# The up projection of the feed-forward layer by seven products instead of eight (hybrid encoder, one core)

## The chip, the cores and the metric

One core of one Trainium2 chip runs the whole program. The metric is the time of one execution on the device, in microseconds (us); lower is better. TensorE (PE in the rows) multiplies matrices, VectorE (DVE), ScalarE (ACT) and GpSimd (POOL) work element by element, SyncE (SP) issues the DMAs. SBUF is the memory next to the engines, PSUM the small one that TensorE writes.

## The reference

Two layers of an encoder with 512 tokens and 1024 features. Each layer has a mixer (three attention branches with gates), and after it a feed-forward part, the one that is changed:

```python
h = rms_norm(x, norm_ffn[l])
x = x + jnp.square(jax.nn.relu(h @ w_ff1[l])) @ w_ff2[l]
```

`w_ff1` is 1024 x 4096 (the up projection), `w_ff2` is 4096 x 1024 (the down projection), all in float32.

## The kernel before, in words

Activations stand feature-major: a tile has 128 features by 512 tokens. Precision is kept by splitting every operand in two: `hi` is the value rounded to the type float32r, `lo` the rest, and a product is three matmuls (hi·hi, hi·lo, lo·hi) that add up in one PSUM bank (`feature_tile`, L331). Each matmul has its own load of 128x128 weights and streams 512 columns.

Weights come through `Stream.take`: one DMA of 512 KB into `raw`, a copy on ScalarE that makes `whi` (L140), a subtraction on VectorE that makes `wlo` (L142). There are three buffers of each.

`merge` makes the output projection: eight tiles `ps_o` of 24 matmuls. As each is done, `x` takes it up (L908), `norm_part` multiplies it by the gain and splits it into `xgh` and `xgl` (L271, L272), and `norm_square` adds its square to `acc` (ScalarE L282, GpSimd L283). The factor per token of the norm is applied later, after the up projection.

`ffn` then runs two halves. A half makes 16 tiles of the up projection (`up`, 24 matmuls each), evacuates each with relu and the factor `rb` (L930), squares it and splits it into `ah` and `al` (L933 to L935), and then makes eight tiles of the down projection, of 48 matmuls each, that are added to `x` (L964). In the first half the sums of the norm (`norm_sums`, `ps_sum`) and its row (`norm_rows`, `ps_r`) are put between the first up tiles.

TensorE runs in the order in which the program is written. The order on the other engines is set by a scheduler from priorities and from a model of when each instruction is ready; `high_priority(30)` moves the making of weights some 30 instructions ahead. Every engine then runs its instructions strictly in that order.

## Time and profile before

| | |
|---|---|
| runs of the kernel | 1854.17, 1857.88 (median), 1862.26 us |
| profiled execution | 1858.96 us, its span 1856.9 us |
| TensorE busy | 1801.5 us, 97% of the span, 8496 matmuls |
| VectorE busy | 1088.9 us, 59% |
| ScalarE busy | 784.5 us, 42% |
| GpSimd busy | 311.4 us, 17% |
| granted TensorE clock | 0.993 of full speed (2.4 GHz) |

The span goes from the first to the last instruction. Busy time of TensorE counts a matmul from its start to its modelled end, so that neighbours overlap; how fast matmuls follow each other is read from their starts, or from a stretch that holds nothing else, divided by their number.

### The profile page before, as it was taken

How to read it: one execution, taken by the hardware profiler on the slowest of the kernel's cores; microseconds unless marked ns; L12 is line 12 of the kernel's file. 1: busy time of each engine (PE TensorE's matmuls, PEld its weight loads, DVE VectorE, ACT ScalarE, POOL GpSimd, SP SyncE). 2: the span in 40 equal slices, each digit the busy share in tenths (PEclk: the TensorE clock that was granted, in tenths of full speed). 3: DMA queues.
4: the chain of work that ended last, by engine and by line, in shares of the span. 5: the costliest groups of instructions: out<-in, count | busy, mean ns of one | idle time of the engine just before them, and what ended most of it. 6: DMA issues, size and time to landing. Idle time of an engine off the chain costs nothing.

```text
span 1856.9 us, 23295 instructions
## 1 busy us (share of the span) xinstructions
PE 1801.5 (97%) x8496; PEld 1495.0 (81%) x8496; DVE 1088.9 (59%) x2223; ACT 784.5 (42%) x1369; POOL 311.4 (17%) x289
## 2 busy tenths in 40 slices
PE   8989989989999999999999899899899999999999
PEld 6778878877888888888887788788778888888887
DVE  7566468488865642454355654684888756334632
ACT  6565456446643221223245644564466433222221
POOL 1442222043101000000124312220431110000000
PEclk9999999999999999999999999999899999999999
DMA  5653365332252333333336533643322533333341
GB/s 180 154 147 105 101 163 138 100 113 69 80 193 80 106 99 98 96 100 110 119 113 158 132 96 109 169 116 110 103 84 80 178 95 97 102 91 102 92 119 62
DMA packets 78850, 211.46 MB, mean 114 GB/s; under 512 B 11392, under 2 KB 14464, under 8 KB 78736
## 3 DMA queue, kind: packets, MB, share of 16 engines
q1 hardware_dynamic: 78736, 209.97, 39.3%
q8 instruction: 67, 1.10, 0.2%
q14 instruction: 47, 0.39, 0.1%
HBM read 172.15 MB, written 12.62 MB: 100 GB/s over the span
## 4 chain that ended last, share of the span: by engine, by line
PE 79%; DVE 8%; ACT 4%; DMA 4%; issue 3%; POOL 2%; SPq 1%; DVEq 0%; ACTq 0%; POOLq 0%
PE ps L331 38%; PE ps_t L366 15%; PE ps_f L331 10%; PE ps_o L331 5%; PE ps_b L776 5%; PE ps_s L662 2%; PE ps_p L689 2%; PE ps_y L700 2%; DMA qq<-nat 2%; DVE pr L677 1%; POOL wlo L142 1%; DVE pr L670 1%; ACT whi L140 1%; DMA cb<-cum 1%; ACT pr L675 1%
## 5 line engine op out<-in xcount | busy, mean ns | idle before, releaser
L140 ACT ACTIVATE whi<-raw 128x1024 fp32r<-128x1024 f32 (+1 forms) x337 | 307.1, 919 | 764.8 <-issue 320.6
L142 DVE TENSOR_TENSOR wlo<-raw,whi 128x1024 fp32r<-128x1024 f32 (+2 forms) x237 | 287.6, 1213 | 232.2 <-ACT whi L140 227.8
L331 PE MATMUL ps<-xgh,whi 128*128 128x512 f32 x512 | 199.4, 389 | 0.0
L331 PE MATMUL ps<-xgh,wlo 128*128 128x512 f32 x512 | 199.2, 389 | 0.0
L331 PE MATMUL ps<-xgl,whi 128*128 128x512 f32 x512 | 199.2, 389 | 0.0
L331 PE MATMUL ps<-ah,whi 128*128 128x512 f32 x512 | 199.2, 389 | 0.0
L331 PE MATMUL ps<-al,whi 128*128 128x512 f32 x512 | 199.2, 389 | 0.0
L331 PE MATMUL ps<-ah,wlo 128*128 128x512 f32 x512 | 199.2, 389 | 0.0
L331 PE MATMUL ps_f<-xgh,whi 128*128 128x512 f32 x464 | 196.2, 423 | 0.0
L331 PE MATMUL ps_f<-xgh,wlo 128*128 128x512 f32 x464 | 182.5, 393 | 0.0
L331 PE MATMUL ps_f<-xgl,whi 128*128 128x512 f32 x464 | 182.5, 393 | 0.0
L142 POOL TENSOR_TENSOR wlo<-raw,whi 128x1024 fp32r<-128x1024 f32 x50 | 121.1, 2422 | 257.0 <-ACT whi L140 234.3
L366 PE MATMUL ps_t<-whi,xgh 128*128 128x512 f32 x384 | 151.2, 394 | 7.0 <-ACT whi L140 7.0
L366 PE MATMUL ps_t<-wlo,xgh 128*128 128x512 f32 x384 | 150.1, 391 | 0.0
L366 PE MATMUL ps_t<-whi,xgl 128*128 128x512 f32 x384 | 149.9, 390 | 0.0
L283 POOL TENSOR_TENSOR acc<-acc,t 128x512 f32<-128x512 f32 x24 | 41.6, 1732 | 518.9 <-ACT t L282 518.9
L331 PEld LDWEIGHTS ps<-ah,whi 128*128 128x128 f32 x512 | 96.1, 188 | 20.1
L331 PEld LDWEIGHTS ps<-xgl,whi 128*128 128x128 f32 x512 | 96.1, 188 | 19.9
L331 PEld LDWEIGHTS ps<-xgh,wlo 128*128 128x128 f32 x512 | 96.1, 188 | 19.9
L331 PEld LDWEIGHTS ps<-al,whi 128*128 128x128 f32 x512 | 96.1, 188 | 19.9
L331 PEld LDWEIGHTS ps<-xgh,whi 128*128 128x128 f32 x512 | 96.1, 188 | 19.9
L331 PEld LDWEIGHTS ps<-ah,wlo 128*128 128x128 f32 x512 | 96.1, 188 | 19.8
(194 smaller groups left out, 3387.0 us busy)
## 6 DMA issues: line engine op xcount, KB each, us to landing
raw<-w SPq DMA_DIRECT2D x277, 512.0 KB, 3.6
qq<-nat SPq DMA_DIRECT2D x64, 128.0 KB, 2.9
kk<-nat SPq DMA_DIRECT2D x64, 128.0 KB, 2.4
kl<-nat SPq DMA_DIRECT2D x64, 128.0 KB, 2.4
gd<-t SPq DMA_DIRECT2D x32, 256.0 KB, 2.2
cb<-cum SPq DMA_DIRECT2D x16, 256.0 KB, 4.0
cb<-gd SPq DMA_DIRECT2D x16, 256.0 KB, 2.7
g<-gd SPq DMA_DIRECT2D x16, 256.0 KB, 4.3
```

The source lines that it names most:

```text
L140: nc.scalar.activation(out=hi[:, c : c + v], in_=raw[:, c : c + v], func=AF.Copy)
L142: k.lo_engine.tensor_tensor(out=lo[:, c : c + w], in0=raw[:, c : c + w], in1=hi[:, c : c + w].bitcast(F32), op=ALU.subtract)
L283: (engine or nc.gpsimd).tensor_tensor(out=self.acc, in0=self.acc, in1=sq, op=ALU.add)
L331: nc.tensor.matmul(out=ps, lhsT=a[:, k], rhs=b[k], start=first and k == 0 and j == 0, stop=last and k == n - 1 and j == 2)
L366: nc.tensor.matmul(out=pss[t][:, 0:width], lhsT=a[k][:, t * P : t * P + P], rhs=b[:, i], start=c == 0 and i == 0 and j == 0, stop=last and ...
L662: nc.tensor.matmul(out=ps[:, 0:n], lhsT=a[:, i * P : (i + 1) * P], rhs=b[:, 0:n], start=j == 0, stop=j == len(terms) - 1)
L670: nc.vector.tensor_tensor_reduce(out=p, in0=ps[:, 0:n], in1=b, scale=1.0, scalar=-3e38 * sign, op0=ALU.add, op1=ALU.max if branch == 2 els ...
L675: nc.scalar.activation(out=p, in_=p, func=AF.Exp, bias=mn, scale=sign, accum_out=ls)
L677: nc.vector.tensor_scalar(out=p, in0=p, scalar1=li, scalar2=None, op0=ALU.mult)
L689: nc.tensor.transpose(ps[:, o + (i - kb) * P : o + (i - kb + 1) * P], pr[:, offs[i] + kb * P : offs[i] + (kb + 1) * P], self.ident)
L700: nc.tensor.matmul(out=yps[:, kb * P : T], lhsT=qkv[2][kb // 2][:, kb % 2, h, :], rhs=head[h][gi][x][:, o : o + T - kb * P], start=gi == 0 ...
L776: nc.tensor.matmul(out=pss[u], lhsT=chunk[a][:, u, k], rhs=y[b][k], start=k == 0 and j == 0, stop=k == 3 and j == 2)
```

## The change

The up projection is done for two tiles (256 output features) at once by Strassen's scheme in Winograd's form: the contraction of 1024 is cut into two halves of 512, the outputs into two tiles of 128, the tokens into two halves of 256. Where eight block products were needed, seven are made, from sums and differences of the blocks, and their results are added up again.

- Weights (`take_pair`): two DMAs of 512 KB bring the four blocks. GpSimd makes four differences of 128x512 (`t1` to `t4`). Seven blocks are split into hi and lo: ScalarE makes one copy of 512 columns (`b11`, in buffers of its own) and three of 1024, VectorE as many subtractions.
- Activations (`norm_pair`, in `merge`): the tiles kt and kt + 4 are paired, and the eight output tiles run in the order 0, 4, 1, 5, 2, 6, 3, 7. For each pair VectorE makes the sums `s1` to `s4` in halves of 256 tokens, and everything is split in hi and lo.
- Products (`pair_products`): 7 x 4 x 3 = 84 matmuls of 256 columns with 128x128 weights each, into four PSUM banks that hold two results each; two sets of four banks alternate. The first pair of a layer runs part by part of the contraction, the others product by product.
- Sums (`pair_sum`): ScalarE copies one result of 256 columns from PSUM, VectorE makes four additions, each with one operand in PSUM, of 512, 512, 256 and 512 columns. ScalarE then makes relu, square and the hi copy of 1024 columns, VectorE the subtraction for lo.
- The factor of the norm is squared and applied after the down projection (one more VectorE operation for each of its tiles). The two halves become four blocks of four pairs: 336 matmuls of 256 columns, then eight down tiles of 24 matmuls.

The number of bytes loaded stays the same.

```diff
--- before.py
+++ after.py
@@ class Stream @@
+    def take_pair(self, pool, *key):
+        k, nc = self.k, self.k.nc
+        raw = [k.pw.tile([P, 1024], F32, tag="raw", name="raw") for _ in range(2)]
+        sums = [pool.tile([P, 1024], F32, tag="tw", name="tw", bufs=2) for _ in range(2)]
+        w = {}
+        def split(names, src, n, tags):
+            hi, lo = (p.tile([P, n], F32R, tag=t, name=t, **b) for p, t, b in tags)
+            nc.scalar.activation(out=hi[:, 0:n], in_=src[:, 0:n], func=AF.Copy)
+            nc.vector.tensor_tensor(out=lo[:, 0:n], in0=src[:, 0:n], in1=hi[:, 0:n].bitcast(F32), op=ALU.subtract)
+            for i, name in enumerate(names):
+                w[name] = tuple(x[:, 512 * i : 512 * i + 512].rearrange("p (k m) -> p k m", m=P) for x in (hi, lo))
+        with k.tc.high_priority(k.ahead):
+            for i in range(2):
+                nc.sync.dma_start(out=raw[i], in_=self.ap[self.layer, :, self.at + 1024 * i : self.at + 1024 * i + 1024])
+            b = [raw[i][:, 512 * j : 512 * j + 512] for i in range(2) for j in range(2)]
+            t = [sums[i][:, 512 * j : 512 * j + 512] for i in range(2) for j in range(2)]
+            sub = lambda out, x, y: nc.gpsimd.tensor_tensor(out=out, in0=x, in1=y, op=ALU.subtract)
+            plain = ((k.pw, "whi", {}), (k.pw, "wlo", {}))
+            summed = ((pool, "twh", dict(bufs=2)), (pool, "twl", dict(bufs=2)))
+            split(["b11"], raw[0], 512, ((pool, "bh", dict(bufs=2)), (pool, "bl", dict(bufs=2))))
+            split(["b21", "b22"], raw[1], 1024, plain)
+            sub(t[0], b[1], b[0])
+            sub(t[1], b[3], t[0])
+            split(["t1", "t2"], sums[0], 1024, summed)
+            sub(t[2], b[3], b[1])
+            sub(t[3], b[2], t[1])
+            split(["t3", "t4"], sums[1], 1024, summed)
...
@@ class Kern @@
+    def norm_pair(self, l, vcol, pool, kt, x):
+        nc = self.nc
+        h2 = T // 2
+        a, b = slice(0, h2), slice(h2, T)
+        g = self.gain(l, vcol + kt)
+        if kt < 4:
+            self.half = self.half if kt else {}
+            t = self.half[kt] = self.tmp()
+            nc.scalar.activation(out=t, in_=x, func=AF.Copy, scale=g)
+            return
+        t = self.half.pop(kt - 4)
+        q = pool.tile([P, 3, h2], F32, tag="sq", name="sq", bufs=1)
+        sub = lambda out, u, v: nc.vector.tensor_tensor(out=out, in0=u, in1=v, op=ALU.subtract)
+        h = self.px.tile([P, T], F32R, tag="xgh", name="xgh")
+        lo = self.px.tile([P, T], F32R, tag="xgl", name="xgl")
+        nc.scalar.activation(out=h, in_=x, func=AF.Copy, scale=g)
+        sub(q[:, 1], t[:, a], t[:, b])
+        nc.vector.scalar_tensor_tensor(out=t[:, b], in0=x[:, b], scalar=g, in1=t[:, b], op0=ALU.mult, op1=ALU.add)
+        sub(q[:, 0], t[:, b], t[:, a])
+        nc.vector.scalar_tensor_tensor(out=q[:, 2], in0=x[:, a], scalar=g, in1=q[:, 0], op0=ALU.mult, op1=ALU.subtract)
+        nc.vector.scalar_tensor_tensor(out=lo, in0=x, scalar=g, in1=h.bitcast(F32), op0=ALU.mult, op1=ALU.subtract)
+        f = {"a12": [y[:, a] for y in (h, lo)], "a22": [y[:, b] for y in (h, lo)]}
+        h = self.px.tile([P, T], F32R, tag="xgh", name="xgh")
+        lo = self.px.tile([P, T], F32R, tag="xgl", name="xgl")
+        nc.scalar.activation(out=h, in_=t, func=AF.Copy)
+        sub(lo, t, h.bitcast(F32))
+        f |= {"a11": [y[:, a] for y in (h, lo)], "s1": [y[:, b] for y in (h, lo)]}
+        h = pool.tile([P, 3, h2], F32R, tag="sh", name="sh", bufs=4)
+        lo = pool.tile([P, 3, h2], F32R, tag="sl", name="sl", bufs=4)
+        nc.scalar.activation(out=h, in_=q, func=AF.Copy)
+        sub(lo, q, h.bitcast(F32))
+        for i in range(3):
+            f[f"s{2 + i}"] = [y[:, i] for y in (h, lo)]
+        self.xf.append(f)
...
@@ def merge @@
-                self.norm_part(l, V_FFN, m, x[m])
-            outs = [out(m) for m in range(KT)]
+                self.norm_pair(l, V_FFN, pool, m, x[m])
+                self.norm_square(m, x[m])
+            self.xf = []
+            outs = [out(m) for m in (0, 4, 1, 5, 2, 6, 3, 7)]
...
+    PRODUCTS = (
+        ("b11", "a11", 0, 0),
+        ("b21", "a12", 1, 0),
+        ("t2", "s2", 1, 1),
+        ("t3", "s3", 2, 0),
+        ("t1", "s1", 2, 1),
+        ("t4", "a22", 3, 0),
+        ("b22", "s4", 3, 1),
+    )
+    def pair_products(self, w, tags, steps):
+        nc = self.nc
+        h2 = T // 2
+        ps = [None] * 4
+        n = len(self.xf)
+        for i, k in steps:
+            stationary, moving, bank, half = self.PRODUCTS[i]
+            if ps[bank] is None:
+                ps[bank] = self.bank(tags[bank], f"ps_w{bank}")
+            out = ps[bank][:, half * h2 : half * h2 + h2]
+            hi, lo = w[stationary]
+            xh, xl = self.xf[k][moving]
+            for j, (a, b) in enumerate(((hi, xh), (hi, xl), (lo, xh))):
+                nc.tensor.matmul(out=out, lhsT=a[:, k], rhs=b, start=k == 0 and j == 0 and i in (0, 1, 3, 5), stop=k == n - 1 and j == 2 and i in (0, 2, 4, 6))
+            yield
+        self.ps = ps
+    def pair_sum(self, ps, z):
+        nc = self.nc
+        h2 = T // 2
+        add = lambda out, x, y: nc.vector.tensor_tensor(out=out, in0=x, in1=y, op=ALU.add)
+        two = lambda x: x.rearrange("p (u t) -> p u t", u=2)
+        p1 = self.tmp()[:, 0:h2]
+        nc.scalar.activation(out=p1, in_=ps[0][:, 0:h2], func=AF.Copy)
+        add(z[:, 0:5:4], two(ps[1]), p1.unsqueeze(1).to_broadcast([P, 2, h2]))
+        add(z[:, 5:7], two(ps[2]), z[:, 4].unsqueeze(1).to_broadcast([P, 2, h2]))
+        add(z[:, 3], ps[2][:, h2:T], z[:, 5])
+        add(z[:, 1:3], two(ps[3]), z[:, 5:7])
+        return z[:, 0:4].rearrange("p (u v) t -> p u (v t)", u=2)
@@ def ffn @@
     def ffn(self, l, x):
         nc = self.nc
         with ExitStack() as ctx:
+            pa = self.pool(ctx, "act", 4)
+            pf = self.pool(ctx, "ffn", 1)
+            take = lambda j: self.streams[l].take_pair(pf, "f1", j)
+            def up(j, w, a):
+                steps = [(i, k) for k in range(4) for i in range(7)] if j == 0 else [(i, k) for i in range(7) for k in range(4)]
+                yield from self.pair_products(w, (("y", "mm", "mm", "mm"), ("s", "s", "pt", "pt"))[j % 2], steps)
+                c = self.pair_sum(self.ps, pf.tile([P, 7, T // 2], F32, tag="z", name="z"))
+                nc.scalar.activation(out=c, in_=c, func=AF.Relu)
+                nc.scalar.activation(out=c, in_=c, func=AF.Square)
+                h, lo = pa.tile([P, 2, T], F32R, tag="ah", name="ah"), pa.tile([P, 2, T], F32R, tag="al", name="al")
+                nc.scalar.activation(out=h, in_=c, func=AF.Copy)
+                nc.vector.tensor_tensor(out=lo, in0=c, in1=h.bitcast(F32), op=ALU.subtract)
+                for u in range(2):
+                    a[0].append(h[:, u])
+                    a[1].append(lo[:, u])
+            def down(q, m, a):
+                ps = self.mm.tile([P, T], F32, tag="mm", name="ps_2")
+                w = self.streams[l].take(1024, "f2", 8 * q, m)
+                yield from self.feature_tile(ps, [c.rearrange("p (k m) -> p k m", m=P) for c in w], *a)
                 t = self.tmp()
+                nc.vector.tensor_tensor(out=t, in0=ps, in1=rb2, op=ALU.mult)
+                nc.vector.tensor_tensor(out=x[m], in0=x[m], in1=t, op=ALU.add)
+                if q == 3:
+                    if l + 1 < DEPTH:
+                        nc.sync.dma_start(out=self.xd[:, m], in_=x[m])
+                        self.norm_part(l + 1, V_MIX, m, x[m])
+                    else:
+                        nc.sync.dma_start(out=self.a["out"][:, m], in_=x[m])
+            w = take(0)
+            for q in range(4):
                 a = ([], [])
+                for j in range(4 * q, 4 * q + 4):
+                    ahead = take(j + 1) if j % 4 < 3 else None
+                    run_all(up(j, w, a))
+                    w = ahead
+                    if j == 0:
+                        self.norm_sums()
+                    if j == 1:
+                        self.norm_rows("mm")
+                        rb2 = self.rb
+                        nc.vector.tensor_tensor(out=rb2, in0=rb2, in1=rb2, op=ALU.mult)
+                if q == 3 and l + 1 < DEPTH:
                     self.norm_begin()
+                downs = [down(q, m, a) for m in range(KT)]
+                for d in downs[0:2]:
+                    for _ in range(6):
+                        next(d)
+                for i, d in enumerate(downs):
+                    if i == 5 and q < 3:
+                        w = take(4 * q + 4)
+                    run_all(d)
...
@@ def chunk_of @@
-        c = pk(i["w_ff1"][l][:, key[1] * P : (key[1] + 1) * P])
+        w = i["w_ff1"][l][:, 2 * key[1] * P : (2 * key[1] + 2) * P]
+        c = np.stack([pk(w[512 * r : 512 * r + 512, P * u : P * u + P]) for r in range(2) for u in range(2)], axis=1)
```

## Rows read from the trace of the kernel before

**Rows 1.** The page of the profile: its span, the busy time of each engine with its share of the span and instructions, and the shares by engine in the chain that ended last.

```profile
span 1856.9 us, 23295 instructions
PE 1801.5 (97%) x8496; PEld 1495.0 (81%) x8496; DVE 1088.9 (59%) x2223; ACT 784.5 (42%) x1369; POOL 311.4 (17%) x289
...
PE 79%; DVE 8%; ACT 4%; DMA 4%; issue 3%; POOL 2%; SPq 1%; DVEq 0%; ACTq 0%; POOLq 0%
```

**Rows 2.** Busy time by stretch: the stretch and its length, then busy us (and instructions) of TensorE, its weight loads, VectorE, ScalarE and GpSimd, the granted clock, the share of the DMA engines and GB/s. In order: first up half, first down half, second up half, second down half of layer 0, and the output projection before them; then the last down half of layer 1.

```profile
578.80:667.38 88.58, 88.58 (x395) 73.29 (x394) 53.47 (x85) 26.53 (x34) 1.79 (x1) 1.00 0.32 95
667.38:754.42 87.04, 87.04 (x385) 72.10 (x384) 26.39 (x26) 17.54 (x18) 0.00 (x0) 1.00 0.32 97
754.42:841.46 87.04, 87.04 (x385) 72.10 (x384) 50.09 (x62) 24.74 (x31) 0.00 (x0) 1.00 0.32 97
841.46:928.50 87.04, 87.04 (x385) 72.10 (x384) 31.04 (x33) 25.43 (x31) 10.78 (x6) 1.00 0.37 115
...
1765.99:1853.20 87.21, 87.20 (x385) 71.88 (x383) 23.95 (x24) 15.38 (x15) 0.00 (x0) 1.00 0.29 88
535.28:578.80 43.52, 43.52 (x194) 36.05 (x192) 23.37 (x28) 17.55 (x24) 10.30 (x6) 1.00 0.35 103
```

**Rows 3.** The timeline of TensorE in a run of matmuls of 384 columns (start in us, time from the first start to the last end, instruction, x how many merged): three starts of the same kind, three matmuls apart.

```profile
376.48 0.51 PE L366 MATMUL ps_t<-whi,st 128*128 128x384 f32 x2
...
377.00 0.51 PE L366 MATMUL ps_t<-whi,st 128*128 128x384 f32 x2
...
377.52 0.51 PE L366 MATMUL ps_t<-whi,st 128*128 128x384 f32 x2
```

**Rows 4.** The timeline of TensorE where three matmuls of 256 columns stand in a row, each with weights of its own, and the start of the matmul behind them.

```profile
440.42 0.52 PE L662 MATMUL ps_s<-st 96*128 96x256 f32 x3
440.78 0.39 PE L331 MATMUL ps_f<-xgh,whi 128*128 128x512 f32 x1
```

**Rows 5.** The weight loads of one group of matmuls (busy us, mean ns of one).

```profile
L331 PEld LDWEIGHTS ps<-xgh,whi 128*128 128x128 f32 x512 | 96.1, 188 | 19.9
```

**Rows 6.** Groups of ScalarE by shape (busy us, mean ns of one, idle before): copies of 1024, 512 and 768 columns, an evacuation of 256 columns from PSUM, and a load of the function table.

```profile
L140 ACT ACTIVATE whi<-raw 128x1024 fp32r<-128x1024 f32 x227 | 240.6, 1061 | 716.8 <-issue 314.4 <-PE ps L331 238.9 <-PE ps_t L366 97.0
L140 ACT ACTIVATE whi<-raw 128x512 fp32r<-128x512 f32 x102 | 61.1, 622 | 27.1 <-PE ps_t L366 20.3 <-issue 6.2 <-DMA raw<-w 0.5
L691 ACT ACTIVATE pth<-ps_p 128x256 fp32r<-128x256 f32 x48 | 17.8, 371 | 10.4 <-PE ps_p L689 10.1
L140 ACT ACTIVATE whi<-raw 128x768 fp32r<-128x768 f32 x4 | 3.4, 846 | 8.0 <-PE ps_t L366 4.4 <-PE ps_f L331 3.7
L432 ACT ACT_TABLE_LOAD x2 | 2.6, 1283 | 0.0
```

**Rows 7.** Groups of VectorE by shape: subtractions of 1024, 512 and 768 columns with both operands in SBUF, and operations with one operand in PSUM on 512 and 256 columns.

```profile
L142 DVE TENSOR_TENSOR wlo<-raw,whi 128x1024 fp32r<-128x1024 f32 x227 | 280.1, 1234 | 224.6 <-ACT whi L140 220.2 <-DMA raw<-w 2.2 <-DMA cb<-rel 2.2
L142 DVE TENSOR_TENSOR wlo<-raw,whi 128x512 fp32r<-128x512 f32 x2 | 1.4, 692 | 0.3 <-ACT whi L140 0.3
L142 DVE TENSOR_TENSOR wlo<-raw,whi 128x768 fp32r<-128x768 f32 x4 | 3.8, 958 | 7.2 <-ACT whi L140 7.2
L964 DVE TENSOR_TENSOR x<-x,ps 128x512 f32<-128x512 f32 x32 | 22.0, 687 | 113.4 <-PE ps L331 113.4
L692 DVE TENSOR_TENSOR ptl<-ps_p,pth 128x256 fp32r<-128x256 f32 x48 | 20.1, 418 | 11.5 <-ACT pth L691 11.2
```

**Rows 8.** Timelines of GpSimd and VectorE in four places where both work: around 405, 550, 386 and 426 us (start us, us, instruction).

```profile
405.14 2.27 POOL L785 TENSOR_TENSOR mg<-mg,cb 128x512 f32<-128x512 f32 x1 [0.69 <-DVE rs_y L250]
406.19 1.24 DVE L252 TENSOR_TENSOR rs_t<-rs_y 128x4 f32<-128x4 f32 x1
407.47 0.16 DVE L253 SCALAR_TENSOR_TENSOR rs_t<-rs_t,mv 128x4 f32<-128x4 f32 x1
...
549.86 1.33 POOL L283 TENSOR_TENSOR acc<-acc,t 128x512 f32<-128x512 f32 x1 [63.19 <-ACT t L282]
549.96 1.78 DVE L272 SCALAR_TENSOR_TENSOR xgl<-x,vec,xgh 128x512 fp32r<-128x512 f32 x1
553.86 0.74 DVE L272 SCALAR_TENSOR_TENSOR xgl<-x,vec,xgh 128x512 fp32r<-128x512 f32 x1
...
385.77 2.38 POOL L785 TENSOR_TENSOR mg<-mg,cb 128x512 f32<-128x512 f32 x1 [8.03 <-DVE cb L784]
385.77 1.22 DVE L142 TENSOR_TENSOR wlo<-raw,whi 128x1024 fp32r<-128x1024 f32 x1
...
425.51 2.85 POOL L142 TENSOR_TENSOR wlo<-raw,whi 128x1024 fp32r<-128x1024 f32 x1
426.01 1.40 DVE L410 SCALAR_TENSOR_TENSOR v<-ps_t,mf,v 128x512 fp32r<-128x512 f32 x2
427.33 0.67 DVE L784 SCALAR_TENSOR_TENSOR cb<-cb,ps_b 128x512 f32<-128x512 f32 x1
```

**Rows 9.** The timeline of the end of the program.

```profile
1852.80 0.39 PE L331 MATMUL ps<-ah,wlo 128*128 128x512 f32 x1
1853.23 0.69 DVE L964 TENSOR_TENSOR x<-x,ps 128x512 f32<-128x512 f32 x1 [10.19 <-PE ps L331]
1853.94 0.33 SPq L970 DMA_DIRECT2D out<-x  x1
```

More of the change, by code (lines that the diff above doesn't have):

```diff
@@ L878, in mixer, with merge @@
         return y
-    def merge(self, l, y, x):
+    def merge(self, l, y, x, pool):
         nc = self.nc
@@ L921, in ffn @@
         with ExitStack() as ctx:
-            pa = self.pool(ctx, "act", 16)
-            xg = self.nx
-            def up(f, out):
-                hi, lo = self.streams[l].take(1024, "f1", f)
-                ps = self.bank("s" if f == 3 else "mm", "ps_1")
-                yield from self.feature_tile(ps, [c.rearrange("p (k m) -> p k m", m=P) for c in (hi, lo)], *xg)
-                t = self.tmp()
-                nc.vector.scalar_tensor_tensor(out=t, in0=ps, scalar=0.0, in1=self.rb, op0=ALU.max, op1=ALU.mult)
-                h = pa.tile([P, T], F32R, tag="ah", name="ah")
-                lo = pa.tile([P, T], F32R, tag="al", name="al")
-                nc.scalar.activation(out=h, in_=t, func=AF.Square)
-                nc.vector.tensor_tensor(out=t, in0=t, in1=t, op=ALU.mult)
-                nc.vector.tensor_tensor(out=lo, in0=t, in1=h.bitcast(F32), op=ALU.subtract)
-                out[0].append(h)
-                out[1].append(lo)
@@ L1003, in run @@
                 x = [px.tile([P, T], F32, name=f"x{kt}") for kt in range(KT)]
-                self.merge(l, y, x)
+                ps = self.pool(xctx, "sums", 1, side="right")
+                self.merge(l, y, x, ps)
                 yctx.close()
```

39 lines of the change are left out of this document (6 added, 33 removed).

## The prediction

> **What bounds the kernel now.** I read the head of the profile page first: TensorE is busy 97% of the span, the next engine (VectorE) 59%, and the chain that ended last lies on TensorE for 79% [rows 1]. So a change counts by what it does to the time of TensorE, unless it makes another engine later than that. Then I asked for the stretches of the feed-forward part. There TensorE has no gaps: a down half of 384 matmuls takes 87.04 us [rows 2], which is 226.7 ns for a matmul of 512 columns; an up half takes the same, and the first up half 1.5 us more for the sums and the row of the norm. The granted clock is 1.00 in all of these stretches, and GpSimd stands still in most of them. The feed-forward part of a layer is thus four times 87 us of a TensorE that never waits, and the 43.52 us of output projection ahead of it are just as dense (192 x 226.7 ns).
>
> **The matmuls.** For 32 pairs in all (16 per layer), 48 matmuls of 512 columns go and 84 of 256 come. That is 7/8 of the columns, but more matmuls, so what counts is how the time of one falls with its columns. The starts of 384 columns are 0.52 us apart for three, 173.3 ns each [rows 3]. Between 226.7 and 173.3 there are 53.3 ns for 128 columns, and what is left at no columns is 13.3 ns. So 256 columns should take 226.7 - 106.7 = 120.0 ns. Three matmuls of 256 columns in a row, each with a weight load of its own, take 0.36 us to the next start [rows 4]: 120 ns again. I take 120.0.
>
> - before: 48 x 226.7 ns = 10.88 us a pair
> - after: 84 x 120.0 ns = 10.08 us a pair
>
> The gain is 0.80 us a pair, 25.6 us for 32. The eighth of the columns that goes is 6 x 213.3 ns = 1.28 us a pair (41 us); the fixed 13.3 ns, paid 36 times more often, takes 0.48 us of it back. Ends, from the rounding of the 0.36 us: 117 ns would give 34 us, 123 ns 18 us.
>
> **The other engines in a pair of 10.08 us.** ScalarE makes for the weights 0.62 + 3 x 1.06, for the result one copy of 256 columns (0.37) and relu, square, copy of 1024 (3 x 1.06): 7.35 us [rows 6]. It fits. The trace of before has no relu on ScalarE. If it needed another function table than square and copy, two loads of 1.28 us a pair would make 9.9 us; I take none, because the copies and squares before run without one.
>
> VectorE makes for the weights 0.69 + 3 x 1.22, for the sums three additions of 0.69 and one of 0.42 out of PSUM, and 1.22 for lo: 4.35 + 2.49 + 1.22 = 8.06 us [rows 7]. GpSimd makes four differences of 512 columns; one takes 1.33 us undisturbed [rows 8], 5.3 us in all. Each fits by itself, but the two get in each other's way. A VectorE operation on four elements takes 0.16 us, and 1.24 us when it comes while GpSimd adds two tiles: it ends as GpSimd ends. A split takes 0.74 us alone and 1.78 us against GpSimd, and GpSimd's addition takes 2.38 us when a VectorE subtraction starts with it [rows 8]. So two operations with both operands in SBUF take turns, whole instruction by whole instruction. An operation with one operand in PSUM is not held up: 0.70 and 0.67 us beside GpSimd's 2.85 us in the same rows. This is the step that decides, since the change moves work to a GpSimd that stood still.
>
> A block of four pairs gives TensorE 4 x 10.08 = 40.3 us. In it three sets of weights are made (the first set of a block is made during the down tiles before), four results are summed, and about three sets of down weights are split. That is on VectorE 3 x 4.35 + 4 x 3.71 + 3 x 1.22 = 31.6 us, on GpSimd 3 x 5.3 = 16 us. If the additions out of PSUM (4 x 2.49 = 10 us) all run beside GpSimd, the two need 47.6 - 10 = 37.6 us and hide. If none does, they need 47.6 us, 7.3 us more than TensorE. Order and waits decide between these; the weights are made a pair ahead, with some 3 us to spare, so I take 0.5 us lost per block, 4 us in eight blocks, and keep 0 and 7.3 us per block as the ends.
>
> At the end of a block the last pair must be summed and split before the down tiles need it: 0.69 + 3 x 1.06 + 1.22 = 5.1 us after its last product. The first two down tiles run on the other three pairs meanwhile, 36 x 226.7 ns = 8.2 us. This hides, with 3 us to spare; without that cover it would cost 5 us eight times.
>
> **The start of each feed-forward part.** In `merge`, `norm_part` (one VectorE split for each tile) gives way to `norm_pair`: for two tiles four operations of 256 columns, two splits of 512 and one of 768, 4 x 0.42 + 0.74 + 0.69 + 0.96 = 4.1 us [rows 7, 8], against 2 x 0.74 us before. With two weight splits and two evacuations that is 7.9 us in the 10.88 us of two output tiles; it fits, though `acc` on GpSimd takes its turns there as well. What is late is the beginning of the first pair. It needs all seven weight blocks in its first quarter (2.5 us), made by four GpSimd differences and four VectorE splits in a stretch where VectorE already works for `norm_pair`. Its last quarter starts after 63 x 0.12 = 7.6 us and needs the activations of the last output tile, whose chain on VectorE is 0.69 + 4.1 us, behind a weight split (1.22) and up to two turns of GpSimd (2.7): 8.7 us. I take 2.5 us lost per layer, with 0 and 6 us (all four differences and one split, 5.3 + 0.7) as the ends.
>
> **Small terms.** The program ends with one VectorE operation and the DMA of the result [rows 9]; now there are two of 0.69 us: +0.7 us. Between the layers the same 0.69 us is hidden, since the first 72 matmuls of the next layer don't need the last tile. The extra operation on each down tile (0.69 us in 5.44 us) lies beside TensorE. The bytes from memory are the same, at a DMA share of about a third [rows 2]. The sums and the row of the norm cost TensorE the same 1.5 us.
>
> **Sum.** -25.6 + 4 + 2 x 2.5 + 0.7 = -15.9 us. The profiled execution took 1858.96 us, so about 1843 us; it stands 1.1 us above the median of 1857.88, from which the forecast is 1842 us.
>
> **The rivals.**
>
> - *All is hidden.* The additions run beside GpSimd and the start is ready in time: -25.6 + 0.7 = -25 us, 1833 us. For it: the 3 us to spare at each step, and 37.6 us against 40.3. Against it: the crowded end of `merge`.
> - *GpSimd and VectorE become the bound (slower).* They run one after the other and a block takes 47.6 us: 8 x 7.3 = 58 us lost, 1858 - 25.6 + 58 + 5 + 0.7 = 1896 us. It decides from 2.5 us per block on, where the gain less the start is used up ((25.6 - 5.7) / 8); that is when only half of the additions overlap (5 of 10 us). For it: the turns [rows 8], and that in a pair where everything is in flight the operations that take turns are 4.35 + 1.22 + 5.3 = 10.9 us, already more than 10.08. Against it: one pair in four is made during down tiles, where VectorE has room. The Trainium skill has a rule that speaks for this rival (GPSIMD Engine Reference, Specifications): GpSimd shares its SBUF interfaces with VectorE, and contends with VectorE instructions that have two SBUF inputs. By it the weight and activation splits collide and the sums don't; the trace agrees, with the 1.78 against 0.74 us above.
> - *In between,* 2 to 2.5 us lost per block, 16 to 20 us in all: 1854 to 1858 us, no change.
> - *The weight loads bind.* Every matmul loads its weights, and one load is shown as 188 ns [rows 5]. If a matmul could not be shorter than that, a pair would take 84 x 188 = 15.8 us, 157 us more in all, 2015 us. Against it: the three matmuls of 256 columns load weights at 120 ns each [rows 4], so most of those 188 ns is not time in which the next must wait. The Trainium skill states a milder form (TensorE: Matmul & The Clock Gate, Back-to-back issue gap): in a stream of loads and matmuls about 81 ns at 128 columns and 131 ns at 512. By the middle of these, an estimate of 98 ns at 256, a pair would go from 6.3 to 8.2 us and the kernel would be some 62 us slower; the trace disagrees already at 512 columns, with 226.7 ns.
>
> **Chances.** Part of it hidden, as in the sum: 0.45, with a range of its own from 1835 to 1849. All hidden: 0.25. In between: 0.12. GpSimd and VectorE bind: 0.15. Weight loads: 0.03. About 0.5% (9.3 us) is what a measurement of this kernel can tell from no change, so faster means below 1848.6 us: both first cases nearly whole, 0.69; the same up to 1867 us takes the rest of the first, the case between and the mild end of the slow one, 0.15; slower 0.16. The range that should hold the time 8 times in 10 goes from 1830 us (all hidden at 119 ns a matmul) to 1865 us (1 us more per block than the point that decides).
>
> **What would show it.** In an up stretch, starts of `ps_w` 120 ns apart and 10.08 us for a pair; more says that the weight loads bind. Idle time of TensorE before the matmuls on `t1` to `t4`, put down to a VectorE split, says that turns with GpSimd are late; idle time at the first down tile of a block, put down to `al`, that the chain of the sums is. VectorE subtractions whose mean is well over 1.22 us count the turns. A down block must stay at 43.5 us, and the output projection too. A table load of ScalarE in each pair would refute the 7.35 us.

## The result, and the profile after

The forecast was wrong, and in its sign: it said 1842 us. The changed kernel takes 1872.12 us (median of 6 runs, 1866.62 to 1876.12) against 1858.43 us before (6 runs, 1854.17 to 1862.26). The ratio is 1.007, with a 95% interval from 1.0053 to 1.0086: slower by 0.7%. The profiled execution took 1869.22 us. Its page answers [rows 1] so (span, busy time of the engines, shares of the chain that ended last):

```profile
span 1867.4 us, 26253 instructions
PE 1789.4 (96%) x9648; PEld 1534.8 (82%) x9648; DVE 1271.7 (68%) x2393; ACT 918.3 (49%) x1513; POOL 518.1 (28%) x417
...
PE 48%; DVE 9%; ACT 3%; issue 3%; DMA 3%; POOL 2%; SPq 0%; DVEq 0%; POOLq 0%; ACTq 0%
```

TensorE is busy for 12 us less, and the span is 10.5 us longer: the loss is for the most part waiting. From the first output tile of a layer to its last down tile the two layers take 7.6 and 9.0 us more than before in the profiled executions, and the end of the program 0.8 us more; the mixers, which the change does not touch, take 2.0 us more in layer 0 and 8.8 us less in layer 1, for a reason that no run shows. So the change itself costs about 17 us there. Where they lie, the stretches of layer 0 show (columns as in [rows 2]): the output projection, the first pair, the second, the third and fourth, the first down block, the second up block, the second down block.

```profile
537.23:580.75 43.52, 43.52 (x193) 36.05 (x192) 31.52 (x42) 21.86 (x31) 9.96 (x7) 1.00 0.26 79
580.75:599.70 18.95, 13.23 (x85) 12.07 (x84) 16.01 (x12) 6.06 (x8) 13.93 (x9) 0.82 0.33 95
600.51:613.90 13.39, 10.57 (x86) 10.16 (x85) 13.05 (x28) 7.80 (x10) 6.55 (x4) 1.00 0.20 55
615.02:635.62 20.60, 20.42 (x170) 20.20 (x168) 15.98 (x18) 9.73 (x14) 8.41 (x4) 1.00 0.33 103
635.62:684.23 48.61, 45.84 (x195) 36.92 (x194) 30.40 (x32) 16.63 (x18) 13.05 (x8) 0.96 0.35 106
684.23:725.24 41.01, 40.82 (x338) 40.41 (x336) 28.01 (x30) 21.68 (x25) 13.36 (x8) 1.00 0.25 80
725.24:768.78 43.54, 43.54 (x194) 36.04 (x193) 29.79 (x31) 14.89 (x16) 12.66 (x8) 1.00 0.39 120
```

From the second up block on all is as forecast: 41.0 us for four pairs (40.3 taken, and 0.5 lost), 43.5 for eight down tiles. The loss is at the start of the layer: the first pair takes 18.95 us instead of 10.08, the second 13.39, and the first down block 48.61 instead of 43.5. From the first output tile to the end of the first down block it is 147.0 us in layer 0 and 147.6 in layer 1; by the terms of the prediction without any loss it would be 43.52 + 4 x 10.08 + 1.5 + 43.52 = 128.9. Call this stretch *the start*: 18 us too long, twice. The experiments are measured by it too, because a whole execution carries a variation of its own: in the eight profiled executions of kernels that change nothing ahead of it (before, the change, E1, E4, E5, E9 to E11) the output projection of layer 0 began between 535.3 and 541.3 us.

TensorE's timeline in the first pair shows three waits (in brackets: the idle time and what ended it), and behind them a lower clock:

```profile
580.87 0.28 PE L1020 MATMUL ps_w<-xgl,bh 128*128 128x256 f32 x1
583.16 0.38 PE L1020 MATMUL ps_w<-xgh,bl 128*128 128x256 f32 x1 [2.02 <-DVE bl L139]
...
585.38 0.38 PE L1020 MATMUL ps_w<-sh,twh 128*128 128x256 f32 x1 [1.48 <-ACT twh L138]
...
588.05 0.58 PE L1020 MATMUL ps_w<-sh,twl 128*128 128x256 f32 x1 [2.09 <-DVE twl L139]
...
591.27 0.41 PE L1020 MATMUL ps_w<-sh,wlo 128*128 128x256 f32 x1
591.49 0.41 PE L1020 MATMUL ps_w<-xgh,bh 128*128 128x256 f32 x1
```

```profile
585.70:592.50 6.80, 4.58 (x20) 4.03 (x19) 6.80 (x7) 3.04 (x4) 4.51 (x4) 0.50 0.30 96
592.50:599.70 7.20, 7.20 (x60) 7.03 (x59) 4.46 (x3) 1.24 (x2) 4.56 (x3) 1.00 0.37 102
```

The waits are 2.02 + 1.48 + 2.09 = 5.6 us. In the second stretch 60 matmuls take 7.20 us, 120 ns each; in the first the clock stands at 0.50 (1.2 GHz), and most starts are 0.21 to 0.22 us apart. So the waits cost a second time: 18.95 - 10.08 - 5.6 = 3.3 us. Of these, 2.3 us are the 18 matmuls from 588.05 to 592.5 us, which take 4.5 us instead of 18 x 0.12; the rest lies mostly around the three waits.

Why are the weights late? First GpSimd, then VectorE in the same stretch:

```profile
578.80 1.29 POOL L356 TENSOR_TENSOR acc<-acc,t 128x512 f32<-128x512 f32 x1 [4.24 <-ACT t L355]
580.05 2.51 POOL L148 TENSOR_TENSOR tw<-raw 128x512 f32<-128x512 f32 x2
582.52 3.39 POOL L148 TENSOR_TENSOR tw<-raw,tw 128x512 f32<-128x512 f32 x2
```

```profile
581.56 3.23 DVE L139 TENSOR_TENSOR bl<-raw,bh 128x512 fp32r<-128x512 f32 x2
584.72 1.49 DVE L331 SCALAR_TENSOR_TENSOR t<-x,vec,t 128x256 f32<-128x256 f32 x1
586.13 0.74 DVE L334 SCALAR_TENSOR_TENSOR xgl<-x,vec,xgh 128x512 fp32r<-128x512 f32 x1
586.79 2.35 DVE L139 TENSOR_TENSOR twl<-tw,twh 128x1024 fp32r<-128x1024 f32 x2
589.06 1.49 DVE L326 TENSOR_TENSOR sq<-t 128x256 f32<-128x256 f32 x1
```

Two things stand here. GpSimd does the differences from 580.05 on, behind the squares, though it stood idle for 4.24 us before. And VectorE pays for turns: an operation of 256 columns takes 1.49 us where 0.42 us stood in [rows 7] (and where the same `sq<-t` takes 0.43 us at 578.16, beside an idle GpSimd), two of 512 columns take 3.23 us where 1.4 would do.

In the second pair, and before the row of the norm (`ps_r`) behind it, TensorE waits for a late weight split and for the factor of the norm, which VectorE makes; in the first down block it waits for the last activations (sum, times, longest):

```profile
PE ps_r L392 <- DVE dg L386: 2.1, 2, 1.8
PE ps_w L1020 <- DVE twl L139: 1.2, 2, 1.0
...
PE ps L404 <- ACT ah L1053: 1.7, 1, 1.7
PE ps L404 <- DVE al L1054: 1.0, 2, 0.8
```

These last two are 2.7 of the 5.1 us that the first down block is too long. The other 2.4 us lie around and behind them, where the granted clock falls again: to 0.71 from 645 to 650 us, 0.96 for the block.

### The profile page after: what moved, and what is told of

Same layout as the page of the kernel before. It is cut to its first block, busy times and chain, and to the rows that moved or that the text cites. A ratio compares the mean times of both kernels' runs of the same rounds, so it can differ in the third digit from the quotient of the medians.

```text
span 1867.4 us, 26253 instructions
## 1 busy us (share of the span) xinstructions
PE 1789.4 (96%) x9648; PEld 1534.8 (82%) x9648; DVE 1271.7 (68%) x2393; ACT 918.3 (49%) x1513; POOL 518.1 (28%) x417
## 3 DMA queue, kind: packets, MB, share of 16 engines
q8 instruction: 76, 1.25, 0.3%
## 4 chain that ended last, share of the span: by engine, by line
PE 48%; DVE 9%; ACT 3%; issue 3%; DMA 3%; POOL 2%; SPq 0%; DVEq 0%; POOLq 0%; ACTq 0%
PE ps L404 18%; PE ps_w L1020 8%; PE ps_t L439 7%; PE ps_f L404 5%; PE ps_b L849 2%; PE ps_o L404 2%; POOL tw L148 2%; DVE z L1028 2%; DMA raw<-w 2%; DVE twl L139 2%; PE ps_s L735 1%; PE ps_y L773 1%; PE ps_p L762 1%; DVE wlo L178 1%; DMA qq<-nat 1%
## 5 line engine op out<-in xcount | busy, mean ns | idle before, releaser
L176 ACT ACTIVATE whi<-raw 128x1024 fp32r<-128x1024 f32 (+3 forms) x273 | 239.1, 885 | 353.6 <-PE ps_t L439 123.2
L178 DVE TENSOR_TENSOR wlo<-raw,whi 128x1024 fp32r<-128x1024 f32 (+3 forms) x173 | 216.1, 1249 | 89.9 <-ACT whi L176 87.6
L148 POOL TENSOR_TENSOR tw<-raw 128x512 f32<-128x512 f32 x64 | 108.6, 1698 | 324.1 <-DMA raw<-w 157.8
L148 POOL TENSOR_TENSOR tw<-raw,tw 128x512 f32<-128x512 f32 x64 | 105.3, 1646 | 68.8 <-DMA raw<-w 67.2
L1064 DVE TENSOR_TENSOR t<-ps,rb 128x512 f32<-128x512 f32 x64 | 44.1, 690 | 101.4 <-PE ps L404 101.4
L748 ACT ACTIVATE pr<-pr,mn 128x512 f32<-128x512 f32 (+3 forms) x128 | 71.6, 559 | 80.8 <-DVE mn L743 75.8
L138 ACT ACTIVATE twh<-tw 128x1024 fp32r<-128x1024 f32 x64 | 65.8, 1052 | 76.7 <-POOL tw L148 45.0
L404 PEld LDWEIGHTS ps_f<-xgh,wlo 128*128 128x128 f32 x464 | 87.1, 188 | 19.8
L765 DVE TENSOR_TENSOR ptl<-ps_p,pth 128x512 fp32r<-128x512 f32 x144 | 85.2, 596 | 24.9 <-ACT pth L764 24.7
```

The source lines that it names most:

```text
L138: nc.scalar.activation(out=hi[:, 0:n], in_=src[:, 0:n], func=AF.Copy)
L148: sub = lambda out, x, y: nc.gpsimd.tensor_tensor(out=out, in0=x, in1=y, op=ALU.subtract)
L176: nc.scalar.activation(out=hi[:, c : c + v], in_=raw[:, c : c + v], func=AF.Copy)
L178: k.lo_engine.tensor_tensor(out=lo[:, c : c + w], in0=raw[:, c : c + w], in1=hi[:, c : c + w].bitcast(F32), op=ALU.subtract)
L404: nc.tensor.matmul(out=ps, lhsT=a[:, k], rhs=b[k], start=first and k == 0 and j == 0, stop=last and k == n - 1 and j == 2)
L748: nc.scalar.activation(out=p, in_=p, func=AF.Exp, bias=mn, scale=sign, accum_out=ls)
```

## The experiments

Three theories of the start at first: **A**, place: `ffn` opens its pool where `merge` has closed its own, so that `twh` and `twl` lie where `mh` and `ml` were, which the output projection reads up to its last matmul; therefore the first pair's weights are queued late. **B**, turns of VectorE and GpSimd. **C**: the last output tile's `norm_pair` stands behind the second pair's weights. The start is the length in layer 0 and layer 1 of one profiled execution.

| kernel | median us | ratio to before, 95% | start, us |
|---|---|---|---|
| the change | 1872.12 | 1.007 (1.0053 to 1.0086) | 147.0, 147.6 |
| E1 second pair later | 1873.19 | 1.0067 (1.0047 to 1.0088) | 147.4, 147.7 |
| E2 early buffers | 1863.72 | 1.002 (1.0007 to 1.0033) | 143.8, 142.2 |
| E3 both | 1864.34 | 1.0023 (1.001 to 1.0037) | 141.5, 141.9 |
| E4 no differences | 1861.46 | 1.0014 (1.0001 to 1.0027) | 141.8, 143.7 |
| E5 differences on VectorE | 1870.18 | 1.0046 (1.0028 to 1.0065) | 139.2, 140.5 |
| E6 = E3 + two `z` | 1854.25 | 0.9976 (0.9962 to 0.999) | 138.4, 138.1 |
| E7 = E6 + order | 1848.47 | 0.994 (0.9924 to 0.9956) | 135.1, 136.0 |
| E8 = E7, no GpSimd at the start | 1842.37 | 0.9905 (0.9889 to 0.992) | 131.0, 131.4 |
| E9 = the change, no GpSimd at the start | 1867.62 | 1.005 (1.0035 to 1.0065) | 144.6, 143.3 |
| E10 = E9 + order | 1864.77 | 1.0028 (1.0012 to 1.0044) | 142.3, 142.0 |
| E11 = E8 less early buffers and E1 | 1850.87 | 0.9961 (0.9945 to 0.9976) | 137.0, 136.2 |
| E12 = E8 with one `z` | 1851.63 | 0.9962 (0.995 to 0.9975) | 136.6, 138.2 |

**E1.** The second pair's weights without their priority:

```diff
...
-        with k.tc.high_priority(k.ahead):
+        with k.tc.high_priority(k.ahead if ahead is None else ahead):
...
-            take = lambda j: self.streams[l].take_pair(pf, "f1", j)
+            take = lambda j: self.streams[l].take_pair(pf, "f1", j, ahead=0 if j == 1 else None)
```

> The weights of the second pair lose their lead of 30 instructions (ahead=0 for j = 1); nothing else changes. In the changed kernel TensorE stands or runs at the half clock in the first block of each layer: the first pair takes 18.95 us instead of 10.08, the second 13.4, the first down block 48.6 instead of 43.5. Theory A (place): the first pair's weight blocks are queued late, behind the last work of the output projection, because their buffers lie in memory that the output projection's operands still hold. Then this edit hardly helps: the waits of 2.0, 1.5 and 2.1 us in the first quarter stay, and the time is within 4 us of 1872. Theory B (turns): VectorE and GpSimd take turns, and 7 us of VectorE's 16.6 us between 581 and 598 us are waiting for GpSimd; then it may help by what the second pair's work takes from the first (2 to 4 us per layer, 1865 to 1868). Theory C (the last activations): norm_pair of the last tile is behind the second pair's weights; then the first pair shortens by 3 to 6 us per layer (1860 to 1866).

The first pair takes 19.6 and 19.7 us, and C by itself has fallen: the last tile's `sl` ends 16.0 us after the pair's first matmul instead of 17.1, and the three waits in the first quarter, for weights, are still there (2.0, 1.5 and 2.2 us in layer 0).

**E2, E3.** The buffers of the sums are there before the output projection; room for them comes from putting `ml` into memory that is free by then. E3 is E1 and E2 together.

```diff
-        sums = [pool.tile([P, 1024], F32, tag="tw", name="tw", bufs=2) for _ in range(2)]
+        sums = [k.pfirst.tile([P, 1024], F32, tag="tw", name="tw", bufs=2) for _ in range(2)]
...
-            summed = ((pool, "twh", dict(bufs=2)), (pool, "twl", dict(bufs=2)))
+            summed = ((k.pfirst, "twh", dict(bufs=2)), (k.pfirst, "twl", dict(bufs=2)))
...
+                self.pfirst = self.pool(xctx, "first", 1, side="right")
```

> The buffers of the differences and of their hi and lo parts (tw, twh, twl) come from a pool that is opened before the output projection, in memory of their own; to make room, the lo parts of the merged tiles go into the memory of merged tiles that are no longer needed, and the gates of the third branch into temporaries. The instructions are the same. Theory A: the differences of the first pair run some 10 us earlier; the waits on twh and twl (1.5 and 2.1 us) go, the wait on bl (2.0 us) may stay; the first pair takes 11 to 14 us instead of 19, the clock does not fall, and the whole is 12 to 26 us faster than the changed kernel: 1846 to 1860 us. Theory B: the turns are only moved into the output projection and the first pair gains 3 us at the most: 1866 to 1872 us. Theory C: the first pair still waits for the last activations, at its last quarter: 15 to 17 us for the first pair, 1862 to 1868 us.

> Both edits, early buffers and no lead for the second pair's weights. If A and C both hold, the first pair takes 11 to 13 us, the second 10 to 11.5, the first down block 43.5 to 45, and the time is 1836 to 1848 us, below the kernel before (1858). If the turns decide (B), it is no better than the better of the two edits alone.

Part of it. E2 lies between what A and what B would have given, and E3 is no better than E2, which was the sign of B. Beside early buffers E1 is worth 2.3 and 0.4 us of the start and nothing in the time. The differences now run as soon as their data are there, as GpSimd's timeline of E6, which has the same buffers, shows:

```profile
560.34 2.09 POOL L148 TENSOR_TENSOR tw<-raw 128x512 f32<-128x512 f32 x1 [1.73 <-DMA raw<-w]
...
564.96 1.60 POOL L148 TENSOR_TENSOR tw<-raw,tw 128x512 f32<-128x512 f32 x1 [1.10 <-DMA raw<-w]
```

That is 20 us earlier than in the change, and the waits for `twh` and `twl` at the first pair are gone. But TensorE now waits for `b11` there; E3's longest waits, from the output projection to the end of the first down block:

```profile
PE ps_w L1021 <- ACT bh L138: 3.2, 1, 3.2
PE ps_w L1021 <- DVE bl L139: 2.1, 1, 2.1
PE ps L404 <- ACT ah L1054: 1.7, 1, 1.7
PE ps L404 <- DVE al L1055: 1.0, 2, 0.8
```

`bh` is copied late (at 583.9 us in E3, where the output projection ends at 581.3) because ScalarE's queue holds operations ahead of it that wait for VectorE's late additions to `x`. And the first down block is as late as before.

**E4.** The four differences of the first two pairs of a layer left out:

```diff
...
+            if key[1] < 2:
+                split(["t1", "t2"], raw[0], 1024, summed)
+                split(["t3", "t4"], raw[1], 1024, summed)
+            else:
...
```

> For the first two pairs of each layer GpSimd's four differences are left out and the loaded blocks are split in their place (so the result of these pairs is not the reference's); splits, products and sums are as many as before. Theory B: without GpSimd in the way VectorE's work in the first 17 us shrinks by about 5 us, the waits on twh and twl go; first pair 11 to 14 us, 1850 to 1860 us. Theory A: hi and lo of these blocks still wait for memory and stand behind the last output tile's work, so the wait on bl stays and those on twh and twl shrink by 2 to 3 us in all: 1862 to 1868 us.

The first pair falls to 16.0 us, the second to 10.1, and the first down block rises to 49.7 and 51.4 us: even with no difference to make, three quarters of the start's loss stay (12.9 + 14.8 of 36.8 us). B by itself can hardly be it; the seven squares are still on GpSimd here, and E9 takes these away too.

**E5.** The opposite: all differences on VectorE.

```diff
-            sub = lambda out, x, y: nc.gpsimd.tensor_tensor(out=out, in0=x, in1=y, op=ALU.subtract)
+            sub = lambda out, x, y: nc.vector.tensor_tensor(out=out, in0=x, in1=y, op=ALU.subtract)
```

> The changed kernel with the four differences of every pair on VectorE instead of GpSimd, nothing else; the result stays the same. Theory B (turns of VectorE and GpSimd are the loss): without GpSimd no VectorE subtraction waits for a turn; VectorE pays 4 x 0.69 = 2.8 us more per pair but gets back some 7 us of turns in the first pair, so the first pair falls from 18.95 to about 14 us, and the kernel to about 1860 us; the up blocks grow a little, since 31.6 + 4 x 2.8 - 1.2 = 42 us of VectorE work now stand against 41 us (1 us in six blocks). Theory A (the weights of the first pair are queued late, since their buffers lie over the output projection's): the first pair stays above 17 us, the first down block at 48 us, the kernel at 1872 us or above.

The first pair takes 17.2 and 16.9 us, nearer to A; the start is 7 to 8 us shorter, as B would have it; and the kernel hardly gains, for a reason that the stretches show (first down block, second up block, second down block):

```profile
631.31:677.06 45.75, 44.16 (x194) 35.97 (x193) 31.66 (x40) 15.15 (x17) 0.00 (x0) 1.00 0.38 114
677.06:717.37 40.31, 40.31 (x337) 40.30 (x336) 28.33 (x36) 21.73 (x25) 0.00 (x0) 1.00 0.26 81
717.37:762.59 45.22, 44.11 (x195) 35.97 (x193) 31.59 (x40) 14.80 (x17) 0.00 (x0) 1.00 0.38 116
```

An up block is now 40.31 us, 120.0 ns a matmul, and nothing is lost: what the up blocks of the change lose (0.7 us and more) goes with GpSimd's differences. But every down block now waits for its last activations and takes 44.7 to 47.5 us, though VectorE is not full (28.3 of 40.3 us in the up block). E12 points to the one `z`; E5 with two was not run. In the steady blocks, with one `z`, GpSimd is worth its turns.

**E6.** Theory D, the one buffer `z`: the sums of a pair wait until `al` of the pair ahead is made. Two buffers, with the temporaries elsewhere:

```diff
-        add(z[:, 0:5:4], two(ps[1]), p1.unsqueeze(1).to_broadcast([P, 2, h2]))
...
+        add(p[:, 1], ps[1][:, h2:T], p[:, 0])
+        add(z[:, 0], ps[1][:, 0:h2], p[:, 0])
...
-                c = self.pair_sum(self.ps, pf.tile([P, 7, T // 2], F32, tag="z", name="z"))
+                c = self.pair_sum(self.ps, pf.tile([P, 4, T // 2], F32, tag="z", name="z", bufs=2))
```

> The third experiment (buffers there before the output projection, second pair's weights later) and two buffers for z, with the temporaries of the sums in the six buffers of 512 columns; VectorE has one addition more per pair (two of 256 columns for one of 512, 0.15 us). Theory D (the lag of the first pair stays in the chain sums - relu - square - copy - subtraction, some 10 us per pair, since the next pair's sums wait for the one buffer z): the first down block falls from 47.2 and 47.6 us to about 44.5, the rest stays, the kernel about 6 us below the third experiment, 1858 us. Rival (the last pair's own chain of 5 us is late behind other VectorE work): the first down block stays above 47 us, the kernel at 1864 us.

The first down block is at its 43.5 us and the waits for `ah` and `al` are gone (E6's stretch):

```profile
631.77:675.34 43.57, 43.57 (x195) 36.01 (x194) 27.72 (x29) 14.77 (x16) 12.66 (x8) 1.00 0.39 119
```

**E7.** The product of `b11` last:

```diff
-                steps = [(i, k) for k in range(4) for i in range(7)] if j == 0 else [(i, k) for i in range(7) for k in range(4)]
+                steps = [(i, k) for k in range(3) for i in range(1, 7)] + [(0, k) for k in range(3)] + [(i, 3) for i in range(7)] if j == 0 else [(i, k) for i in range(7) for k in range(4)]
```

> The sixth kernel, and in the first pair of a layer the product of b11 is made behind the six others (first three quarters of the contraction, then its three quarters, then the last quarter of all). Theory A2 (the start waits for bh and bl, 3.2 and 2.1 us, because the copy of b11 stands behind other ScalarE work): those waits go, and output projection and first pair together fall from 61.3 us to about 57 us, the kernel by 8 us against the sixth, to 1850 us. Rival (what the last quarter needs, the activations of the last output tile, is ready no earlier, since VectorE and GpSimd have more to do in the output projection than it lasts: 36 us of VectorE and 14.6 us of GpSimd for 43.5 us): the wait moves to the last quarter, the two together stay within 1 us of 61.3, the kernel within 3 us of the sixth.

Between the two forecasts: output projection and first pair take 58.9 and 59.8 us, where E6 has 62.2 and 61.9. The waits for `bh` and `bl` are gone, and a new one is there (E7's waits in the start):

```profile
PE ps_w L1021 <- DVE x L982: 3.3, 2, 2.7
PE ps_r L392 <- DVE dg L386: 0.5, 2, 0.3
```

L982 is the addition of an output tile to `x`. It has to read its PSUM bank before `ps_w` can use that bank, and it is late on a crowded VectorE.

**E8.** Nothing on GpSimd from the output projection to the second pair:

```diff
-            sub = lambda out, x, y: nc.gpsimd.tensor_tensor(out=out, in0=x, in1=y, op=ALU.subtract)
+            sub = lambda out, x, y: (nc.vector if key[1] < 2 else nc.gpsimd).tensor_tensor(out=out, in0=x, in1=y, op=ALU.subtract)
...
-                self.norm_square(m, x[m])
+                self.norm_square(m, x[m], nc.vector)
```

> The seventh kernel, and GpSimd does nothing from the output projection to the second pair: the differences of the first two pairs of a layer and the seven additions for the squares of the norm are made by VectorE. VectorE then has 36 + 7 x 0.69 + 4 x 0.69 = 43.6 us in the 43.5 us of the output projection, with no turns, against 36 + 14.6 us less the additions out of PSUM (5.5 us) = 45.1 us before. Theory B (turns): output projection and first pair fall by 2 to 5 us per layer against the seventh, the kernel by 4 to 10 us. Rival (VectorE is simply full): no gain or a loss of up to 3 us per layer.

The kernel is faster than the change and than the kernel before, by 0.95% against before (0.8 to 1.1). Its stretches: the whole start, the first pair, the first down block.

```profile
541.03:671.98 130.95, 129.49 (x732) 113.74 (x730) 105.97 (x155) 64.47 (x80) 29.20 (x16) 1.00 0.36 108
...
584.55:594.90 10.35, 10.32 (x86) 10.12 (x84) 9.80 (x19) 4.27 (x7) 0.00 (x0) 1.00 0.30 88
...
628.43:671.98 43.55, 43.55 (x195) 36.04 (x193) 27.75 (x29) 14.76 (x16) 12.48 (x8) 1.00 0.40 119
```

Is it the turns, or only that VectorE makes a difference faster than GpSimd? The output projection, in E7 and then in E8, tells:

```profile
534.63:578.15 43.52, 43.52 (x193) 36.04 (x192) 37.48 (x43) 21.70 (x29) 17.21 (x10) 1.00 0.33 97
...
541.03:584.55 43.52, 43.52 (x194) 36.04 (x193) 37.12 (x56) 25.14 (x34) 0.00 (x0) 1.00 0.33 97
```

VectorE does 13 operations more in E8 and is busy for 37.12 us instead of 37.48: in E7 ten of its operations are lengthened, by some 9 us in all, in E8 none. It is the turns; and the addition to `x`, for which TensorE waited in E7, is in time.

**E9 to E12** take E8 apart. E9 has E8's two lines alone, E10 these and the order.

> The changed kernel, and GpSimd does nothing from the output projection to the second pair (differences of two pairs and additions of the squares on VectorE); buffers, z and order as in the changed kernel. If turns are the whole loss of the start, output projection and first pair fall from 62.5 us to about 55 us, the first down block to 44 us, the kernel to about 1848 us. If the place of the buffers binds as well, the two stay at 59 us or more, the first down block at 46 us or more, and the kernel at 1860 us or more.

> The ninth kernel with the product of b11 last in the first pair. If the place of the buffers does not bind once the turns are gone, output projection and first pair fall to about 54.5 us as in the eighth kernel; if it binds, what the first quarter waits for is twh and twl and not bh, so the order brings under 1 us and the two stay at 58 us or more. Kernel: 1845 against 1860 us.

In both the place binds: the first pair still takes 15.5 to 16.9 us, and it waits for `twh` and `twl`.

> The eighth kernel (1842.4 us) without its early buffers and without the later second pair: two buffers for z, order, no GpSimd at the start. Place binds: output projection and first pair 57 us or more against 54, the kernel at 1848 us or more. Place does not bind: 1842 us.

Place binds: 60.8 and 60.0 us for output projection and first pair, against 53.9 and 54.3 in E8. E11's waits of the products in the start are those of the change again, less `bl`:

```profile
PE ps_w L1020 <- DVE twl L139: 2.1, 2, 1.3
PE ps_w L1020 <- ACT twh L138: 1.4, 1, 1.4
```

(E11 also gives back E1's priority. E1 alone did nothing, and E2 against E3 gives it 2.3 and 0.4 us of the start beside early buffers, so most of the 6.0 and 4.8 us between E11 and E8 is the buffers'; how much, in E8 itself, was not run.)

> The eighth kernel (1842.4 us) with one buffer for z as in the change. If the one buffer only passes on the lag of the start, and the start is now in time, the first down block stays at 43.6 us and the kernel at 1843 us; if the buffer itself costs at the start of a layer, where the norm's row stands between the pairs, the first down block goes back to 46 us or more and the kernel to 1847 us or more.

The buffer itself costs, even with a first pair that is in time (10.4 and 10.8 us): the first down block takes 49.2 and 50.3 us. My idea in E6 that it only passes on a lag of the start has fallen. VectorE's timeline of E12 shows how (some of the sums `z` and the subtractions `al`, first to fourth pair):

```profile
594.92 0.41 DVE L1029 TENSOR_TENSOR z<-ps_w,z 128x256 f32<-128x256 f32 x1
...
602.06 1.22 DVE L1055 TENSOR_TENSOR al<-z,ah 128x1024 fp32r<-128x1024 f32 x1
...
605.47 0.69 DVE L1029 TENSOR_TENSOR z<-ps_w,t 128x512 f32<-128x512 f32 x1
...
616.85 1.22 DVE L1055 TENSOR_TENSOR al<-z,ah 128x1024 fp32r<-128x1024 f32 x1
618.11 0.69 DVE L1029 TENSOR_TENSOR z<-ps_w,t 128x512 f32<-128x512 f32 x1
...
623.95 1.23 DVE L1055 TENSOR_TENSOR al<-z,ah 128x1024 fp32r<-128x1024 f32 x1 [3.37 <-ACT ah L1054]
625.28 0.69 DVE L1029 TENSOR_TENSOR z<-ps_w,t 128x512 f32<-128x512 f32 x1
```

The first pair's products end at 588.0, its `al` at 603.3, 15 us later: between its sums VectorE's queue holds weight splits and the small operations of the norm's factor, which only the first block has. The second pair's sums begin after that, at 605.5, and its `al` ends at 618.1. With one buffer a pair needs from 618.11 to 625.28, 7.2 us, one after the other, even where VectorE does nothing else in between; against TensorE's 10.08 that makes up 3 us a pair, too little before the down tiles come.

## Why the prediction was wrong, and where it was right

The step that failed is the term *the start of each feed-forward part*: 2.5 us taken, 0 and 6 as ends, and 18.1 and 18.7 us measured (147.0 and 147.6 less 128.9). It accounts for the miss: 36.8 us instead of 6 (twice 2.5, and 0.5 for each of the two first blocks), where the forecast is 30 us below the result. Both signs that the prediction named, waits for `twl` and for `al`, came, but only there. In layer 0 the 18.1 us are 8.9 in the first pair, 3.3 in the second up to the row of the norm, 5.1 in the first down block, and the rest between. Sentence by sentence:

- "With two weight splits and two evacuations that is 7.9 us in the 10.88 us of two output tiles; it fits": it was summed for VectorE alone. For the whole output projection VectorE has 36 us (eight weight splits, eight additions, four times 4.1 us, and the first pair's splits) and GpSimd 14.6 us (seven squares at 1.33 and 5.3 us of differences); less the 5.5 us of additions out of PSUM, which overlap, this is by estimate 45.1 us taking turns in 43.5. I had set up this sum for an up block, and not here. Without GpSimd at the start (E7 to E8) the start falls by 4.1 and 4.6 us.
- "It needs all seven weight blocks in its first quarter": the right place, and the waits there, 5.6 and 5.4 us, are within the upper end of 6, which has all four differences made while TensorE stands. The 2.5 us taken supposed that they are begun in time. They weren't: their buffers were not free. Early buffers bring 3.2 and 5.4 us alone (E2), 6.0 and 4.8 us, with E1, where all else is mended (E11 to E8). What `b11`'s place in the order costs, 3.3 and 2.1 us (E6 to E7), shows only then.
- "The first two down tiles run on the other three pairs meanwhile, 36 x 226.7 ns = 8.2 us. This hides, with 3 us to spare." True of the six later down blocks, 43.5 to 43.7 us each. False of the two first, which take 48.6 and 48.1 us: the 5.1 us of the last pair's chain begin late, since `z` has one buffer. Two buffers bring 5.6 and 6.8 us (E12 to E8).
- "The sums and the row of the norm cost TensorE the same 1.5 us": 0.81 and 1.12 us, and 1.8 us of waiting ahead of the row, since VectorE is late with the factor.
- Nothing in the prediction said that a wait also lowers the clock; in the first pair what came on top of the waits was another 3.3 us, and some of the 5.1 us in the first down block.

What held:

- The 120.0 ns a matmul: 40.31 us for 336 in E5. The weight loads don't bind; that rival would have taken 15.8 us a pair. By the Trainium skill (TensorE: Matmul & The Clock Gate, Back-to-back issue gap) the estimate for 256 columns was 98 ns, on a line through 81 ns at 128 columns and 131 ns at 512 (and not their middle, which is 106); the trace disagrees, with 120.0.
- 0.5 us lost in a block to turns: the three later up blocks of layer 0 take 41.0 to 41.2 us, those of layer 1 41.2 to 41.5, 0.9 us lost on the mean. The slow rival, GpSimd and VectorE as the bound of every block at 1896 us, didn't come; GpSimd's differences take 1.65 to 1.70 us where 1.33 us were undisturbed, and that fits. By the Trainium skill (GPSIMD Engine Reference, Specifications) GpSimd shares its SBUF interfaces with VectorE and contends with VectorE instructions that have two SBUF inputs: the trace agrees, at the start above all (1.49 us for 256 columns).
- The tail: one operation of 0.69 us more, as the end of the program shows.

```profile
1863.00 0.69 DVE L1064 TENSOR_TENSOR t<-ps,rb 128x512 f32<-128x512 f32 x1 [4.02 <-PE ps L404]
1863.72 0.69 DVE L1065 TENSOR_TENSOR x<-x,t 128x512 f32<-128x512 f32 x1
```

- ScalarE loads no function table in the feed-forward parts.

With the start mended (E8) it takes 131.0 and 131.4 us, 2.1 and 2.5 us lost, and the kernel at 1842.37 us stands where the forecast did. That doesn't make the forecast right: it priced the kernel of the diff, and E8 has five edits more.

## What to carry to other kernels

Here a scheme that saves matmuls paid in the steady part and was billed at its start. Look there first: add up what all engines that take turns have to do in the stretch that precedes it, and see whether the new buffers are free by then. Count one buffer as a chain: with `z` alone the next sums begin when the last subtraction ends, and a lag shrinks only by the difference of the two pitches (10.08 less 7.2 us). Mend such causes together: E1, E2, E4, E5 and E9 each go at one and leave the kernel slower than before, while the five edits of E8 together (E1, early buffers, two `z`, order, no GpSimd at the start) bring 30 us.

## What the runs showed of the hardware that was not expected

- Waiting has a second price: while and after TensorE waited three times, for 5.6 us in all, the granted clock stood at a half (585.7 to 592.5 us), and 5.6 us of waits cost 8.9 us in the first pair (2.3 of the 3.3 us on top are matmuls at that clock). In E8, where it hardly waits, the clock is 1.00 through the whole start.
- A busy GpSimd lengthens short VectorE operations most: 256 columns by a factor of up to 3.5 (1.49 to 0.42 us; the eight `sq<-x,vec,sq` take 1.25 us on the mean, and 0.48 in E8), 1024 columns on the mean by 14% (`twl` 1.39 us in the change, 1.22 us in E5), as the groups of the change and then of E5 show (busy us, mean ns of one).

```profile
L139 DVE TENSOR_TENSOR twl<-tw,twh 128x1024 fp32r<-128x1024 f32 x64 | 88.3, 1392 | 13.2 <-ACT twh L138 13.2
```

```profile
L139 DVE TENSOR_TENSOR twl<-tw,twh 128x1024 fp32r<-128x1024 f32 x64 | 77.1, 1220 | 15.1 <-ACT twh L138 14.3
```
